# Keeping the split gated outputs of the left half of an output projection for the right half

## Chip, cores and metric

One core of a Trainium2 chip runs the whole kernel in one launch. The metric is the device time of one execution in microseconds (us); lower is better. Engines are named as in the profile: PE (TensorE, matmuls), PEld (its weight loads), DVE (VectorE), ACT (ScalarE), POOL (GpSimd), SP (SyncE, which here issues the DMAs).

## What is computed

A backbone of four layers over 1024 latent tokens and 256 context tokens of width 1024, all in float32. Cut to what matters here:

```python
for i in range(DEPTH):                      # 4 layers, mixers A, B, C, A
    need_ctx = i < DEPTH - 1
    h = rms_norm(x, norm_g[i]) * (1.0 + sc[:, None]) + sh[:, None]
    u, z = jnp.split(h @ w_in, [n_mix_cols], axis=-1)
    ...
    o, oc = mixer(u, uc, ...)               # attention of one of three kinds
    x = x + gt[:, None] * ((o * jax.nn.silu(z)) @ w_out)
    if need_ctx:
        xc = xc + gtc * ((oc * jax.nn.silu(zc)) @ w_out)
```

The last line pair is the output projection: the gated mixer output `o * silu(z)`, 1024 features for each token, times `w_out` (1024 x 1024), times a gate, added to the residual.

## The kernel before

Matmuls run in a reduced float32 form (`F32R`) with each operand split into a high part, rounded to that form, and a low part, the rest. A product is three matmuls: high by high, high by low, low by high (`PROD`, line 372). A split costs one rounding on POOL (`round_pool`, line 130) and one subtraction on DVE (`sub`, line 133).

Every layer has the same stages: projection of the normalised rows to queries, keys, values and gates; attention; output projection (`out_proj`, line 861), which also makes the normalised and modulated rows of the next layer. A layer's gated outputs lie in blocks `og`, features in the partitions. The projection treats tiles of 128 tokens: ten in the first three layers (eight of latent tokens, two of context), eight in the last. It goes through the list `work` (line 904): first the left 512 output columns (h = 0) of all tiles, then the right 512 (h = 1) of all tiles. For each entry:

- `start(i + 1)` splits the gated output of the next entry's tile into two buffers `ogt` (high, low; `parts`, line 901, `split`, line 885), in four blocks: four roundings on POOL, four subtractions on DVE.
- `load` brings the residual rows `xo`, two entries ahead.
- `products` (line 894) runs 24 matmuls of 512 columns into one PSUM bank `y`: eight slices of features by three products.
- With h = 1, in the layers but the last, the transposes of the tile before (`transposed`, line 287, eight matmuls `xT` from `xn`) and its modulation (`modulate`, line 297) follow: four operations `hs` on ACT, four on DVE, then the split of the result for the next layer, `hhi` on POOL and `hlo` on DVE.
- The tile's end: `yg` (DVE, line 934) multiplies by the gate, POOL adds the residual (line 935), a DMA stores it. With h = 1 `norm_rows` (line 279) then squares and sums the rows on ACT (`junk`, line 284), takes the power -1/2 on POOL (`rsqrt`, `rstd`, lines 140 and 146) and scales on DVE (`xn`, line 285).

After the fourth entry from the end the first weights of the next layer are loaded (`wraw`), and split behind the last products (`whi` on POOL, `wlo` on DVE). The transposes of the last tile come after the first pair of the next layer's projections (`proj`, line 382).

Buffers in SBUF come from two pools: 42 "whole" buffers of 1024 elements a partition and 12 "half" ones of 512. A scheduler gives out buffers and sets each engine's order from the order of the code; the function `in_order` pins parts of it. Each engine works its own queue in order.

Of the kernel before, what the change touches and what calls it, by code (L numbers as in the profile page):

```python
# [22 lines left out]
KT = D // P  # L23
# [49 lines left out]
class Net:  # L73
# [787 lines left out]
    def out_proj(self, l, wop, steps, og, tiles):  # L861

        nc = self.nc
        last = l == self.depth - 1
        gts, late = {}, []
        self.new_h()
        new = {t: self.block_rows(self.out, t) if last else self.dram([P, D], name="xres") for t in tiles}

        def load(h, t):
            s = 0 if t < 8 else 1  # L870
            cs = slice(h * 512, h * 512 + 512)
            if s not in gts:
                gts[s] = self.slot([P, D], name="gt")
                g = self.gate[l]
                self.dma(gts[s], bass.AP(tensor=g.tensor, offset=g.offset + s * D, ap=[[0, P], [1, D]]))
            if h == 0 or last:
                full = x = self.slot([P, 512], name="xo")
            else:
                full = self.slot([P, D], name="xo")
                self.dma(full[:, :512], new[t][..., :512])  # L880
                x = full[:, cs]
            self.dma(x, self.xres[t][..., cs])
            return full, x

        def split(t, blocks, ot):

            g, o = t // 4, (t % 4) * P
            for b in blocks:
                a = og.block(b, g)[:, :, o : o + P]
                hi, lo = (x[:, 2 * b : 2 * b + 2, :] for x in ot)  # L890
                self.round_pool(hi, a)
                self.sub(lo, a, hi)

        def products(ps, h, ot, ks):
            for k in ks:
                for j, (a, b) in enumerate(self.PROD):
                    nc.tensor.matmul(  # L897
                        ps, ot[a][:, k, :], wop[h](b, k), start=(k == 0 and j == 0), stop=(k == KT - 1 and j == 2)
                    )

        def parts():
            return [self.slot([P, KT, P], F32R, "ogt") for _ in range(2)]

        work = [(h, t) for h in range(2) for t in tiles]
        ready = [load(*work[0]), load(*work[1])]
        halves = {}

        def start(i):
            ot = parts()
            split(work[i][1], range(4), ot)  # L910
            halves[i] = ot

        start(0)
        for i, (h, t) in enumerate(work):
            cs = slice(h * 512, h * 512 + 512)
            if i < len(steps):
                steps[i]()
            if i + 1 < len(work):
                start(i + 1)
            if i + 2 < len(work):  # L920
                ready.append(load(*work[i + 2]))
            full, x = ready.pop(0)
            ps = self.pb("y")
            products(ps, h, halves.pop(i), range(KT))
            while self.tail:
                self.tail.pop(0)()
            if i + 1 == len(work) and not last:
                for step in splits:
                    step()
            if late:  # L930
                xn, tt = late.pop(0)
                self.modulate(self.transposed(xn), tt, self.mod[l + 1])
            y = self.slot([P, 512], name="yg")
            nc.vector.tensor_tensor(y, ps, gts[0 if t < 8 else 1][:, cs], op=ALU.mult)
            nc.gpsimd.tensor_tensor(x, x, y, op=ALU.add)
            self.dma(new[t][..., cs], x)
            if h == 0 or last:
                continue
            xn = self.slot([P, D], name="xn")
            self.norm_rows(xn, full)  # L940
            late.append((xn, t))
            if i == len(work) - 4:
                self.first_w, loads, splits = self.weight_blocks(*self.first_block(l + 1))
                for x in loads:
                    x()
        self.pending = [
            lambda xn=xn, tt=tt: self.modulate(self.transposed(xn), tt, self.mod[l + 1]) for xn, tt in late
        ]
        for t in tiles:
            self.xres[t] = new[t]  # L950
# [767 lines left out]
```

## Time and profile before

| what | us |
|---|---|
| median of 3 runs | 3666.45 |
| lowest and highest run | 3665.51, 3667.39 |
| the profiled execution, its own time | 3671.03 |
| span of its trace, first to last instruction | 3669.2 |
| PE busy in the span | 3518.5 (96%) |
| DVE, ACT, POOL busy | 2153.7, 1323.0, 1998.8 |

The profile is one execution. A row gives an engine, a line of the kernel, the operation, what it writes and reads (`out<-in`), and times. "Idle before" is the time the engine stood still just ahead of an instruction, with the instruction that ended the wait behind the arrow. The ends of matmuls are modelled, so consecutive matmuls overlap in the rows; their distance in time is read from start to start.

### The profile page before, as it was taken

The numbers are of one execution on the slowest core, as the hardware profiler recorded it, in microseconds if no ns is written. First come the engines' busy times: TensorE is split into PE (matmuls) and PEld (weight loads), VectorE is DVE, ScalarE is ACT, GpSimd is POOL, SyncE is SP. The second block draws the span as 40 slices with busy tenths as digits, with TensorE's granted clock in tenths as the row PEclk, the third lists the DMA queues.
The fourth block names the chain that finished last, engine by engine and source line by source line (L and its number), as shares of the span: only waits on it lengthen the run. The fifth ranks groups of instructions, "written<-read, shape, count | busy, mean of one in ns | idle before, by whom it ended". The sixth has DMA issues, their size and how long they took to land.

```text
span 3669.2 us, 50527 instructions
## 1 busy us (share of the span) xinstructions
PE 3518.5 (96%) x18594; PEld 2615.8 (71%) x18594; DVE 2153.7 (59%) x3675; ACT 1323.0 (36%) x2756; POOL 1998.8 (54%) x2006
## 2 busy tenths in 40 slices
PE   7999999998899999999999999999989999999989
PEld 4887444446788888887778888888877787544447
DVE  5542555565742412888766510899995754566655
ACT  3221444441321212774222211677761221344430
POOL 5540656678631310667765510567776743477786
PEclk9999999999999999999999999999999999999989
DMA  6352543513244444552425432221313334111112
GB/s 208 78 135 83 158 130 103 182 55 97 96 116 138 104 126 111 166 151 69 138 78 137 130 117 61 82 87 38 98 40 99 110 93 125 46 46 37 46 39 86
DMA packets 229459, 370.39 MB, mean 101 GB/s; under 512 B 34088, under 2 KB 124120, under 8 KB 229212
## 3 DMA queue, kind: packets, MB, share of 16 engines
q1 hardware_dynamic: 228636, 367.01, 34.1%
q8 instruction: 148, 2.42, 0.3%
q14 instruction: 99, 0.81, 0.1%
q10 hardware_dynamic: 576, 0.15, 0.0%
HBM read 270.36 MB, written 96.57 MB: 100 GB/s over the span
## 4 chain that ended last, share of the span: by engine, by line
PE 68%; DVE 16%; POOL 9%; issue 4%; DMA 2%; ACT 1%; SPq 0%; POOLq 0%; ACTq 0%; DVEq 0%
PE proj L382 21%; PE zT L467 11%; PE o L725 8%; PE y L897 6%; PE st L700 5%; PE st L701 4%; PE sl L653 3%; DVE ml L1450 3%; PE o L1120 2%; POOL rstd L146 2%; DVE wlo L133 2%; DVE ogt L133 1%; PE qkT L437 1%; POOL hhi L130 1%; POOL p L739 1%
## 5 line engine op out<-in xcount | busy, mean ns | idle before, releaser
L739 POOL TENSOR_TENSOR p<-p,p 128x1024 f32<-128x1024 f32 x224 | 540.1, 2411 | 326.1 <-PE o L725 287.4
L382 PE MATMUL proj<-whi,hhi 128*128 128x512 f32 x1408 | 556.7, 395 | 3.2 <-POOL whi L130 1.9
L382 PE MATMUL proj<-wlo,hhi 128*128 128x512 f32 x1408 | 551.3, 392 | 3.9 <-DVE wlo L133 3.8
L382 PE MATMUL proj<-whi,hlo 128*128 128x512 f32 x1408 | 551.1, 391 | 0.0
L660 DVE TENSOR_REDUCE M<-sl 128x1 f32<-128x512 f32 x512 | 326.8, 685 | 292.5 <-PE sl L653 292.5
L705 ACT ACTIVATE p<-st 128x1024 f32<-128x1024 f32 (+1 forms) x336 | 324.4, 1003 | 314.8 <-PE st L701 303.1
L897 PE MATMUL y<-whi,ogt 128*128 128x512 f32 x1216 | 389.7, 398 | 16.7 <-POOL ogt L130 13.1
L133 DVE TENSOR_TENSOR wlo<-wraw,whi 128x1024 fp32r<-128x1024 f32 x136 | 213.5, 1584 | 217.8 <-POOL whi L130 193.0
L725 PE MATMUL o<-p,v 128*64 128x512 f32 x1344 | 324.5, 605 | 1.7 <-DVE M L660 1.1
L130 POOL TENSOR_SCALAR whi<-wraw 128x1024 fp32r<-128x1024 f32 x136 | 179.0, 1321 | 254.0 <-DMA wraw<-in_c_w_in_dram 91.3
L382 PEld LDWEIGHTS proj<-wlo,hhi 128*128 128x128 f32 x1408 | 265.8, 189 | 58.9 <-DVE wlo L133 6.0
L382 PEld LDWEIGHTS proj<-whi,hhi 128*128 128x128 f32 x1408 | 265.8, 189 | 57.5 <-POOL hhi L130 2.4
L382 PEld LDWEIGHTS proj<-whi,hlo 128*128 128x128 f32 x1408 | 265.6, 189 | 55.4
L897 PEld LDWEIGHTS y<-whi,ogt 128*128 128x128 f32 x1216 | 230.7, 190 | 73.2 <-POOL ogt L130 16.8
L467 PE MATMUL zT<-hhi,whi 128*128 128x512 f32 (+1 forms) x704 | 256.6, 365 | 5.9 <-DVE qklo L133 5.6
L404 ACT ACTIVATE y<-proj 128x1024 f32<-128x1024 f32 (+1 forms) x68 | 65.5, 964 | 527.4 <-PE proj L382 470.0
L467 PE MATMUL zT<-hhi,wlo 128*128 128x512 f32 (+1 forms) x704 | 254.3, 361 | 1.3 <-DVE wlo L133 1.3
L467 PE MATMUL zT<-hlo,whi 128*128 128x512 f32 (+1 forms) x704 | 254.2, 361 | 0.0
L897 PE MATMUL y<-wlo,ogt 128*128 128x512 f32 x608 | 239.6, 394 | 0.0
L146 POOL TENSOR_TENSOR rstd<-rstd,mhalf 128x16 f32<-128x16 f32 (+3 forms) x132 | 230.8, 1748 | 10.9
L700 PE MATMUL st<-q,k 128*128 128x512 f32 x512 | 218.3, 426 | 2.3 <-ACT p L705 2.3
L410 DVE TENSOR_TENSOR y<-y,rstd 128x1024 f32<-128x1024 f32 (+1 forms) x68 | 104.1, 1531 | 193.0 <-POOL rstd L146 193.0
(221 smaller groups left out, 7242.7 us busy)
## 6 DMA issues: line engine op xcount, KB each, us to landing
adaw<-in_ada_w_dram SPq DMA_DIRECT2D x96, 512.0 KB
xo<-xres SPq DMA_DIRECT2D x86, 256.0 KB
wraw<-in_a_w_in_dram SPq DMA_DIRECT2D x40, 512.0 KB
k<-k SPq DMA_DIRECT2D x40, 512.0 KB
q<-qkhi SPq DMA_DIRECT2D x76, 256.0 KB
q<-qklo SPq DMA_DIRECT2D x76, 256.0 KB
q<-q SPq DMA_DIRECT2D x136, 128.0 KB
wraw<-in_b_w_in_dram SPq DMA_DIRECT2D x32, 512.0 KB
```

Of the source, the lines that this page charges most:

```text
L130: self.nc.gpsimd.tensor_scalar(out=out, in0=in_, scalar1=1.0, scalar2=0.0, op0=ALU.mult, op1=ALU.add)
L133: self.nc.vector.tensor_tensor(out, a, b, op=ALU.subtract)
L146: nc.gpsimd.tensor_tensor(r, r, self.mhalf[:, :n], op=ALU.pow)
L382: nc.tensor.matmul(ps[:, i, :], self.h_op(a, 2 * tp + i, k), wop(b, k), start=(k == 0 and j == 0), stop=(k == KT - 1 and j == 2),)
L467: nc.tensor.matmul(ps, wop(a, k)[:, b * P : (b + 1) * P], self.h_cols(c, g, k), start=(k == 0 and j == 0), stop=(k == KT - 1 and j == 2),)
L660: nc.vector.tensor_reduce(out=o, in_=st["ps", hh], axis=AX.X, op=ALU.max)
L700: nc.tensor.matmul(ps[:, hh, :], self.k_op(K, 0, kt), q1[:, hh, :], start=True, stop=False)
L701: nc.tensor.matmul(ps[:, hh, :], self.k_op(K, 1, kt)[0 : HD + 1], q2[:, hh, :], start=False, stop=True)
L705: nc.scalar.activation(p, ps, AF.Exp, scale=HD**-0.5)
L725: nc.tensor.matmul(st["o"][hh * HD : (hh + 1) * HD, :], v(hh, kt), p[:, hh, :], start=j == 0, stop=j == N - 1, tile_position=(0, hh * HD),)
L739: eng.tensor_tensor(a, a, p, op=ALU.add)
L897: nc.tensor.matmul(ps, ot[a][:, k, :], wop[h](b, k), start=(k == 0 and j == 0), stop=(k == KT - 1 and j == 2))
```

## The change

In the left half each tile's split is made once and its two buffers are kept, by the tile's number; the right half reads them again and then lets them go. Ahead of the change each entry of `work` made its own split, so every tile was split twice. For ten tiles up to 20 whole buffers are held at the turn from left to right.

```diff
         def start(i):
-            ot = parts()
-            split(work[i][1], range(4), ot)
-            halves[i] = ot
+
+            t = work[i][1]
+            if t not in halves:
+                halves[t] = parts()
+                split(t, range(4), halves[t])
...
-            products(ps, h, halves.pop(i), range(KT))
+            products(ps, h, halves[t] if h == 0 else halves.pop(t), range(KT))
```

The change's name also speaks of the differential layer's bias; the diff has no line on it. After the change lines from 914 on stand two lower in the file.

The orders of PE and ACT stay as they are. The first place is DVE's queue in the right half of the first layer, between the norm of the third tile and the end of the fourth (`xn`, normalised rows; `ogt`, split of the gated output `og`; `yg`, gated product; `hs`, modulated rows of the tile before). Before:

```order
L285 TENSOR_SCALAR xn_7274<-xo_7080,rstd_7278 128x1024
L133 TENSOR_TENSOR ogt_7283<-og_618,ogt_7282 128x256
L133 TENSOR_TENSOR ogt_7283<-og_621,ogt_7282 128x256
L133 TENSOR_TENSOR ogt_7283<-og_623,ogt_7282 128x256
L133 TENSOR_TENSOR ogt_7283<-og_626,ogt_7282 128x256
L934 TENSOR_TENSOR yg_7347<-y_7295,gt_6603 128x512
L305 TENSOR_SCALAR hs_7330<-xT_7325,colA_589,colS_590 128x128 x4
L133 TENSOR_TENSOR hlo_7178<-hs_7330,hhi_7177 128x2x128
```

The same place now:

```order
L285 TENSOR_SCALAR xn_7234<-xo_7060,rstd_7238 128x1024
L936 TENSOR_TENSOR yg_7297<-y_7245,gt_6603 128x512
L305 TENSOR_SCALAR hs_7280<-xT_7275,colA_589,colS_590 128x128 x4
L133 TENSOR_TENSOR hlo_7148<-hs_7280,hhi_7147 128x2x128
L133 TENSOR_TENSOR hlo_7152<-hs_7280,hhi_7151 128x2x128
```

The four subtractions between `xn` and `yg` are gone; nothing else moved.

The second place is POOL's queue in the same half, from the residual add (`xo`) of the eighth tile on (`rstd`, its norm's factor; `hhi`, the high part of the seventh tile's modulated rows). Before:

```order
L935 TENSOR_TENSOR xo_7446<-xo_7446,yg_7671 128x512
L130 TENSOR_SCALAR ogt_7606<-og_619 128x256 x2
L130 TENSOR_SCALAR ogt_7606<-og_624 128x256 x2
L140 TENSOR_SCALAR rstd_7679<-ss_7677 128x1
L146 TENSOR_TENSOR rstd_7679<-rstd_7679,mhalf 128x1
L130 TENSOR_SCALAR hhi_7493<-hs_7654 128x2x128
L130 TENSOR_SCALAR hhi_7501<-hs_7654 128x2x128
L130 TENSOR_SCALAR hhi_7497<-hs_7654 128x2x128
L130 TENSOR_SCALAR hhi_7505<-hs_7654 128x2x128
L130 TENSOR_SCALAR ogt_7683<-og_619 128x256 x2
L130 TENSOR_SCALAR ogt_7683<-og_624 128x256 x2
```

The same place now:

```order
L937 TENSOR_TENSOR xo_7376<-xo_7376,yg_7581 128x512
L140 TENSOR_SCALAR rstd_7589<-ss_7587 128x1
L146 TENSOR_TENSOR rstd_7589<-rstd_7589,mhalf 128x1
L130 TENSOR_SCALAR hhi_7423<-hs_7564 128x2x128
L130 TENSOR_SCALAR hhi_7431<-hs_7564 128x2x128
L130 TENSOR_SCALAR hhi_7427<-hs_7564 128x2x128
L130 TENSOR_SCALAR hhi_7435<-hs_7564 128x2x128
L937 TENSOR_TENSOR xo_7451<-xo_7451,yg_7645 128x512
```

Two splits of four roundings are gone here. The factor `rstd` of the eighth tile still stands ahead of the `hhi` of the seventh, as it did; at the other tiles `hhi` of the tile before comes first, or three of its four parts.

## Rows read from the trace of the kernel before

**Rows 1.** The page, engines: busy us, share of the span, instructions.

```profile
PE 3518.5 (96%) x18594; PEld 2615.8 (71%) x18594; DVE 2153.7 (59%) x3675; ACT 1323.0 (36%) x2756; POOL 1998.8 (54%) x2006
```

**Rows 2.** Groups of instructions, 923.44 to 1006 us: busy, mean ns, idle before.

```profile
L130 POOL TENSOR_SCALAR ogt<-og 128x256 fp32r<-128x256 f32 x32 | 17.9, 584 | 0.0
```

**Rows 3.** Waits of PE, 923 to 1006 us: total, times, longest.

```profile
PE xT L293 <- DVE xn L285: 9.0, 9, 1.7
```

**Rows 4.** Windows: stretch, length, busy of each engine, PE clock, DMA, GB/s.

```profile
929.67:976.63 46.96, 39.70 (x195) 31.54 (x194) 38.89 (x85) 16.17 (x37) 36.10 (x66) 1.00 0.38 118
976.63:983.75 7.12, 6.78 (x33) 5.20 (x33) 7.12 (x16) 2.30 (x7) 6.30 (x13) 1.00 0.62 225
...
1781.64:1828.61 46.97, 39.66 (x195) 31.54 (x194) 38.89 (x85) 16.17 (x37) 36.11 (x66) 1.00 0.37 119
1828.61:1836.67 8.06, 8.06 (x32) 6.42 (x33) 8.06 (x18) 2.30 (x7) 6.30 (x13) 0.79 0.54 194
...
2834.38:2881.34 46.96, 39.66 (x195) 31.54 (x193) 38.89 (x85) 16.16 (x37) 36.09 (x66) 1.00 0.37 119
2881.34:2888.45 7.11, 6.76 (x32) 5.20 (x33) 7.11 (x16) 2.31 (x7) 6.30 (x13) 1.00 0.60 216
...
3608.80:3663.40 54.60, 54.56 (x241) 44.86 (x239) 24.17 (x42) 0.00 (x0) 29.11 (x40) 1.00 0.31 92
```

**Rows 5.** Timeline of PE, right half of the first layer: start us, us.

```profile
928.65 0.39 PE L897 MATMUL y<-whi,ogt 128*128 128x512 f32 x1
...
929.67 0.48 PE L897 MATMUL y<-whi,ogt 128*128 128x512 f32 x1
...
983.75 0.48 PE L897 MATMUL y<-whi,ogt 128*128 128x512 f32 x1
...
989.09 0.39 PE L897 MATMUL y<-whi,ogt 128*128 128x512 f32 x1
...
1005.03 1.09 PE L293 MATMUL xT<-ident,xn 128*128 128x128 f32 x8 [1.68 <-DVE xn L285]
```

**Rows 6.** Timeline of all engines, 943.1 to 952.6 us.

```profile
943.03 0.39 PE L897 MATMUL y<-whi,ogt 128*128 128x512 f32 x1
...
943.19 0.89 DVE L285 TENSOR_SCALAR xn<-xo,rstd 128x1024 f32<-128x1024 f32 x1
944.01 2.01 DVE L133 TENSOR_TENSOR ogt<-og,ogt 128x256 fp32r<-128x256 f32 x4
...
945.94 0.68 DVE L934 TENSOR_TENSOR yg<-y,gt 128x512 f32<-128x512 f32 x1
...
946.70 1.29 POOL L935 TENSOR_TENSOR xo<-xo,yg 128x512 f32<-128x512 f32 x1 [1.29 <-DVE yg L934]
...
948.02 1.06 ACT L284 ACTIVATE junk<-xo 128x1024 bf16<-128x1024 f32 x1 [1.68 <-POOL xo L935]
...
950.04 0.61 POOL L146 TENSOR_TENSOR rstd<-rstd,mhalf 128x1 f32<-128x1 f32 x1
...
950.68 0.89 DVE L285 TENSOR_SCALAR xn<-xo,rstd 128x1024 f32<-128x1024 f32 x1
```

**Rows 7.** Timelines of ACT, POOL and DVE, 977 to 998 us.

```profile
977.29 1.49 ACT L314 ACTIVATE hs<-xT,colS,colA 128x128 f32<-128x128 f32 x4
...
979.01 1.68 POOL L130 TENSOR_SCALAR hhi<-hs 128x256 fp32r<-128x256 f32 x4
979.82 2.21 DVE L133 TENSOR_TENSOR hlo<-hs,hhi 128x256 fp32r<-128x256 f32 x4
...
988.79 6.45 POOL L130 TENSOR_SCALAR whi<-wraw 128x1024 fp32r<-128x1024 f32 x4
...
990.31 7.56 DVE L133 TENSOR_TENSOR wlo<-wraw,whi 128x1024 fp32r<-128x1024 f32 x4
```

**Rows 8.** The weight loads' issue (timeline of SP), and a window behind them.

```profile
971.26 1.96 SPq L123 DMA_DIRECT2D wraw<-in_b_w_in_dram  x4
...
984.00:992.00 8.00, 6.81 (x33) 5.17 (x32) 7.26 (x13) 3.12 (x9) 7.18 (x10) 1.00 0.09 33
```

## The prediction

> **What bounds the kernel now.** I began with the page: TensorE (PE) is busy for 96% of the span [rows 1], so time can come only from the places where PE stands still, or from shorter PE work; this change takes no matmul away. Next came the groups of instructions in the first layer's right half. GpSimd (POOL) spends 17.9 us there on 32 roundings of the gated output, 584 ns each [rows 2]; the rest of the removed work is as many VectorE (DVE) subtractions. Busy time off PE costs nothing by itself, so the third view is PE's own waits in the same stretch: nine times PE stands before the transposes of a normalised row tile, 9.0 us in all, and each time DVE's `xn` ends the wait [rows 3].
>
> I call the right half's row tiles R0 to R9 (in the last layer R0 to R7). From the start of R2 to the start of R8 each of the first three layers takes 46.96 or 46.97 us for six tiles, 7.83 us a tile [rows 4]. What PE needs for one: from the first to the last of 24 matmuls behind transposes 983.75 to 989.09, 5.34 us; from the last matmul of a tile over eight transposes to the next tile's first, without a wait, 928.65 to 929.67, 1.02 us [rows 5]. That is 6.36 us. So 1.47 us of each tile is idle PE or its restart. The last layer has no norm behind its right half: there PE is busy for 54.56 of 54.60 us although the splits run [rows 4].
>
> The timeline of one tile shows the loop [rows 6]. `xn` of R2 ends at 944.08; DVE then runs four subtractions of the split for 2.01 us; only then, at 945.94, comes `yg` of R3, whose last product had ended at 943.42. From there: POOL adds to the residual (946.70), ACT squares (948.02), POOL's power ends at 950.65, `xn` of R3 ends at 951.57, and one tile later the same subtractions follow. From `yg`'s start to `xn`'s end it is 5.63 us. The loop `xn`, split, `yg`, `xn` closes in 7.49 us (943.19 to 950.68), longer than PE's 6.36.
>
> **The change, part by part.**
>
> *Splits of the right half removed.* 38 tiles (10, 10, 10, 8) times four blocks: 152 roundings on POOL and 152 subtractions on DVE, some 0.58 us and 0.5 us each [rows 2, 6]; 89 and 76 us of engine time, of which only what stands in the loop counts. The last layer's 32 of each go for nothing: PE covers them. In the other layers the loop loses its 2 us on DVE. `yg` can then start when its products end. I add the steps anew for the chain, from the end of a tile's products: `yg` 0.7, add until 2.1, ScalarE's modulation of the tile before until the same 2.1 (its transposes now start together with `yg`), square until 3.4, POOL's four `hhi` until 3.9, `rstd` until 4.8, `xn` until 5.7 to 5.9. PE asks for these transposes 6.36 after the products' end. The chain fits with about 0.5 to spare, and PE becomes the bound. Six intervals at 6.36 are 38.2 us; 46.96 less 38.2 is 8.8 us a layer, three times **26.4 us**.
>
> *One place where it does not fit.* The order rows of POOL show the `rstd` of R7 ahead of the `hhi` of R6, and ScalarE squares R7 before it modulates R6. From the end of R7's products: add until 2.1, square until 3.4, `rstd` until 4.4, four `hhi` (1.68) until 6.1, the last `hlo` (four take 2.21, the last needs the last `hhi`) about 7.0, `xn` 7.9 [rows 7]. PE asks at 6.36 and waits about 1.6. With some 0.2 of restart R8 to R9 takes 8.2 us. It took 7.12, 8.06 and 7.11 [rows 4], so **2.3 us are lost** here. What hid this was the wait of R8 for its split, which goes.
>
> *The end of the layer.* The next layer's weight splits on POOL (`whi`) began at 988.79, 0.7 us before R9's products ended (989.09 plus 0.39) [rows 5, 7]. In the sum above POOL is free for them 12.6 after the end of R7's products, and R9's products end at 14.6, so they begin 2.0 before. The chain behind them (four `whi`, four `wlo` for 7.56 us, then R9's `yg` to `xn`) ends with the transposes at 1005.03, for which PE waits; it moves with them. I take 1.2 us a layer, **3.6 us**.
>
> *Buffers held longer.* Two buffers of 4 KB a partition for each tile stay taken from the left half to the right: 20 of the 42 whole buffers where 4 were. Nothing in the trace of before prices this. Below, it is 0: by the buffer addresses of the built program, the next layer's four weight loads, issued at 971.26 in R7 [rows 8], take buffers last read no later than R6's products. Elsewhere the orders of buffers are as before, but for one load of residual rows in the first layer's left half, which has to wait a microsecond or two longer, for rows used two tiles on. Above, it is the price of the slower rival below. I take 0, since the addresses say so.
> The Trainium skill (Perfetto Trace Analysis, Identifying Performance Opportunities) says that one gap which repeats on the engine that should be saturated can mean too little SBUF for the next tile. By that rule this gap would grow, and the sum would be the slower rival's 3683; the row with `xn` as releaser of all nine waits speaks against it, so I keep the sum below.
>
> *Moved rows.* On POOL one `hhi` and a rope product change places twice; on the SP queue some residual loads pass stores of the same stage. The loads are issued two or three tiles (over 12 us) ahead of their use, and their place changes by one or two issues: 0. PE's and ScalarE's orders are untouched. The title's second half, on the differential layer, has no line in the diff: 0.
>
> *Sum.* 26.4 - 2.3 + 3.6 = 27.7 us. The profiled execution took 3671.03, the median of the runs is 3666.45, 4.6 less; the same work lies in both, so the profiled time would be 3643.3 and the median **3638.8 us**.
>
> **The rivals.**
>
> *More than that, 3626 us.* Every wait in the stretch goes, the end of the layer too. From R2's start to R9's transposes the first layer takes 75.36 us (929.67 to 1005.03). Eight tiles at 6.36 and 48 projection matmuls at 0.23 (5.34 over 23) are 61.9: 13.5 a layer, 40.5 in all. For it: DVE operations may run shorter once POOL has less to do. Against it: the order at R7, and `wlo`'s 7.56 us, both of which stay.
>
> *Half of it, 3652 us.* The chain comes out at 7.0 instead of 5.9, because the modulation of the tile before no longer runs ahead of `yg` and its eight operations and eight splits now queue in the chain. Six intervals at 7.0 plus restart 0.2 save 3.8 a layer, 11.3; plus 3.6 at the layers' ends and less about 1 at R8 that is 14. For it: the overlap with the tile before is new. Against it: at R3 the measured 5.63 already holds the same `hhi` and `hlo` between add and `xn`.
>
> *Slower, 3683 us.* The held buffers run out: the next layer's weight loads wait until R9's products are done. They were issued at 971.26, and the DMA engines were down to a share of 0.09 in 984 to 992 [rows 8], so they take about 13 us. Then `whi` starts 13 us behind the end of R9 in place of 0.7 ahead, and PE has nothing else: 13.7 in three layers, 41, against the 24 gained, 17 us more. It decides from the point where one of the four loads takes a buffer read after R8. For it: the count is near 42 in that stretch. Against it: the addresses.
>
> *No change.* The idle time at the transposes moves to another engine's wait of the same size, or the change does less than its title says. For it: only its first half is in the diff, and PE is at 96%. Against it: the loop above.
>
> **How the numbers follow.** A measurement of this kernel tells about 0.2%, 7.3 us, from no change. Forecast 0.64, more 0.14, half 0.13, no change 0.05, slower 0.04. Faster is the sum of the first three, 0.91; within 0.2% 0.05; slower 0.04. The range goes from the first rival to just past the second, 3626 to 3653; the last two rivals and the far ends lie outside.
>
> **What would show it.** In the changed profile: POOL's and DVE's `ogt` groups at 152 each; PE's waits for `xn` in the first layer's right half down from nine to about two (R7's transposes, about 1.6, and R9's, under 2); R2 to R8 at 38 to 39 us in each of three layers; `yg` starting within 0.1 of its products' end; the last layer's right half still at 54.6. The prediction is wrong if R2 to R8 stays above 42 us (the chain, not the split, was the bound), if PE waits for weights at the next layer's start (buffers), or if the gain appears there and is lost in the next layer's projections.

## The result, and the profile after

The changed kernel took **3636.26 us** (median of 4 runs, 3634.91 to 3639.78) against 3666.76 of the kernel before beside it: ratio 0.9919, 95% interval 0.9902 to 0.9936, 30.5 us less. The profiled execution took 3635.89, its span is 3634.2. The forecast was 3638.8 in a range of 3626 to 3653. One later run, of the kernel that splits the last layer twice, took 11907.82 us and is left out of that kernel's median.

The page of the changed kernel, engines (to set beside [rows 1]):

```profile
PE 3504.5 (96%) x18594; PEld 2615.1 (72%) x18594; DVE 2070.9 (57%) x3523; ACT 1322.5 (36%) x2756; POOL 1918.5 (53%) x1854
```

DVE lost 152 instructions and 82.8 us of busy time, POOL 152 and 80.3. These 163 us bought 30, and the views below say where. First the groups of instructions of the whole span, the split alone (304 of each before):

```profile
L133 DVE TENSOR_TENSOR ogt<-og,ogt 128x256 fp32r<-128x256 f32 x152 | 90.3, 654 | 10.4 <-POOL ogt L130 10.4
L130 POOL TENSOR_SCALAR ogt<-og 128x256 fp32r<-128x256 f32 x152 | 90.1, 620 | 0.0
```

PE's waits in 923 to 1000 us, the first layer's right half and the next layer's start (total, times, longest; before [rows 3]):

```profile
PE xT L293 <- DVE xn L285: 2.8, 2, 1.7
PE proj L382 <- DVE wlo L133: 0.5, 1, 0.5
```

Nine waits became two: before the transposes of R7 and of R9. The windows from R2 to R8 and from R8 to R9 of each of the three layers, and the last layer's whole right half (columns as in [rows 4]):

```profile
924.42:962.54 38.12, 38.12 (x196) 32.01 (x194) 28.04 (x61) 15.80 (x36) 22.81 (x42) 1.00 0.45 137
962.54:970.26 7.72, 6.58 (x35) 5.25 (x34) 4.61 (x11) 2.70 (x7) 3.91 (x8) 1.00 0.66 247
1767.31:1805.42 38.11, 38.11 (x195) 32.00 (x193) 28.03 (x61) 15.80 (x36) 22.82 (x42) 1.00 0.41 137
1805.42:1813.15 7.73, 6.58 (x36) 5.25 (x34) 4.62 (x11) 2.70 (x7) 3.91 (x8) 1.00 0.69 249
2807.73:2845.79 38.06, 38.06 (x195) 31.98 (x194) 28.03 (x61) 15.80 (x36) 22.82 (x42) 1.00 0.43 138
2845.79:2853.53 7.74, 6.55 (x35) 5.26 (x34) 4.62 (x11) 2.70 (x7) 3.92 (x8) 1.00 0.66 245
3584.54:3628.22 43.68, 43.68 (x193) 35.85 (x191) 5.53 (x8) 0.00 (x0) 10.30 (x8) 1.00 0.28 79
```

From R2 to R8 PE's busy time now equals the length of the window: six tiles at 6.35 us with nothing idle. The timeline of one tile, all engines, shows the loop that was 7.49 us long [rows 6]:

```profile
936.15 0.39 PE L897 MATMUL y<-whi,ogt 128*128 128x512 f32 x1
...
936.58 0.69 DVE L936 TENSOR_TENSOR yg<-y,gt 128x512 f32<-128x512 f32 x1 [0.84 <-PE y L897]
...
937.35 1.29 POOL L937 TENSOR_TENSOR xo<-xo,yg 128x512 f32<-128x512 f32 x1 [2.40 <-DVE yg L936]
...
938.67 1.06 ACT L284 ACTIVATE junk<-xo 128x1024 bf16<-128x1024 f32 x1
...
940.69 0.61 POOL L146 TENSOR_TENSOR rstd<-rstd,mhalf 128x1 f32<-128x1 f32 x1
...
941.34 0.76 DVE L285 TENSOR_SCALAR xn<-xo,rstd 128x1024 f32<-128x1024 f32 x1
...
942.71 1.03 PE L293 MATMUL xT<-ident,xn 128*128 128x128 f32 x8
```

DVE now waits for PE (0.84 before `yg`), no longer PE for DVE. `xn` ends at 942.10, 0.6 before PE asks for it at 942.71. The one place that did not fit, R7, from its last product on (the timeline, rows of PE, DVE, POOL and ACT, R6 and R7):

```profile
962.71 1.29 POOL L937 TENSOR_TENSOR xo<-xo,yg 128x512 f32<-128x512 f32 x1 [2.38 <-DVE yg L936]
964.04 1.06 ACT L284 ACTIVATE junk<-xo 128x1024 bf16<-128x1024 f32 x1 [5.19 <-POOL xo L937]
965.09 1.49 ACT L314 ACTIVATE hs<-xT,colS,colA 128x128 f32<-128x128 f32 x4
965.55 0.55 POOL L146 TENSOR_TENSOR rstd<-rstd,mhalf 128x1 f32<-128x1 f32 x1
966.07 1.68 POOL L130 TENSOR_SCALAR hhi<-hs 128x256 fp32r<-128x256 f32 x4
967.42 1.28 DVE L133 TENSOR_TENSOR hlo<-hs,hhi 128x256 fp32r<-128x256 f32 x3 [0.30 <-POOL hhi L130]
968.62 0.74 DVE L285 TENSOR_SCALAR xn<-xo,rstd 128x1024 f32<-128x1024 f32 x1
969.41 1.09 PE L293 MATMUL xT<-ident,xn 128*128 128x128 f32 x8 [1.14 <-DVE xn L285]
973.97 6.46 POOL L130 TENSOR_SCALAR whi<-wraw 128x1024 fp32r<-128x1024 f32 x4
975.60 0.39 PE L897 MATMUL y<-whi,ogt 128*128 128x512 f32 x1
```

R7's factor `rstd` is there at 966.10, but `xn` stands behind `hlo`, `hlo` behind `hhi` of R6, and those behind ACT's `hs`, which queue behind the square of R7. The last two rows show the layer's end: `whi` begins 2.0 before R9's products end.

### The profile page after: what moved, and what is told of

Its sections match the earlier page's. It is cut to its first block, busy times and chain, and to the rows that moved or that the text cites. A ratio compares the mean times of both kernels' runs of the same rounds, so it can differ in the third digit from the quotient of the medians.

```text
span 3634.2 us, 50186 instructions
## 1 busy us (share of the span) xinstructions
PE 3504.5 (96%) x18594; PEld 2615.1 (72%) x18594; DVE 2070.9 (57%) x3523; ACT 1322.5 (36%) x2756; POOL 1918.5 (53%) x1854
## 4 chain that ended last, share of the span: by engine, by line
PE 73%; DVE 13%; POOL 7%; issue 3%; DMA 2%; ACT 1%; SPq 0%; POOLq 0%; DVEq 0%; ACTq 0%
PE proj L382 21%; PE zT L467 12%; PE y L897 9%; PE o L725 8%; PE st L700 5%; PE st L701 4%; PE sl L653 3%; DVE ml L1452 3%; PE o L1122 2%; DVE wlo L133 1%; POOL rstd L146 1%; PE qkT L437 1%; POOL p L739 1%; PE ada L195 1%; PE pT L1200 1%
```

## The experiments

Medians are compared with the changed kernel's 3636.26 us; a second set of its runs, below, gave 3637.50, so a few us between two kernels can't be told from none. The windows tell more: in two traces of the same kernel those of a stretch agree within 0.1. The sets of runs were made on different chips; the kernel before, run beside each of them, took 3666.76, 3667.21, 3668.22 and 3668.25.

**POOL's roundings back.**

```diff
+            elif not last:
+                again = self.slot([P, KT, P], F32R, "oga")
+                for b in range(4):
+                    self.round_pool(again[:, 2 * b : 2 * b + 2, :], halves[t][0][:, 2 * b : 2 * b + 2, :].bitcast(F32))
```

> The changed kernel, with the four POOL roundings per tile of the right half put back (layers 0 to 2) at their old places, from the kept high part into a buffer that nothing reads. Extra work without use: 30 tiles x 4 roundings of 584 ns, 70 us of POOL. Theory (what went from the loop is DVE's four subtractions between xn and yg; POOL's roundings lay beside it): R2 to R8 stays at 38 to 39.5 us a layer, and the time is 0 to 4 us above the changed kernel's. Rival (POOL's queue was the bound, its load of 36.1 us of 47 with the waits in it): R2 to R8 goes back to 44 to 47 us, and the time is 18 to 27 us above the changed kernel's.

3643.13 us, 6.9 above the changed kernel. The window from R2 to R8 of the first layer:

```profile
929.34:967.73 38.39, 38.39 (x195) 31.86 (x194) 29.07 (x61) 15.77 (x36) 32.81 (x63) 1.00 0.44 137
```

Two of its groups of instructions in 925 to 965 us:

```profile
L130 POOL TENSOR_SCALAR oga<-ogt 128x256 fp32r<-128x256 f32 x24 | 12.0, 523 | 0.0
L285 DVE TENSOR_SCALAR xn<-xo,rstd 128x1024 f32<-128x1024 f32 x6 | 5.4, 892 | 3.8 <-POOL rstd L146 3.5
```

Ten us of POOL work came back and the six tiles took 0.3 us more: POOL alone was not the bound, as the theory had it. The time went a little above its 0 to 4: up to R9's transposes the last two layers, whose PE clock is undisturbed, cost 1.1 us each, mostly from R8 to R9 (8.56 for 7.73), and the first 1.2; the other half of the 6.9 is not placed, and can be the spread of the medians. One number was not expected: `xn` takes 0.89 again, as before the change, where the changed kernel has 0.76.

**DVE's subtractions back.**

```diff
+            elif not last:
+                again = self.slot([P, KT, P], F32R, "oga")
+                for b in range(4):
+                    c = slice(2 * b, 2 * b + 2)
+                    self.sub(again[:, c, :], halves[t][1][:, c, :].bitcast(F32), halves[t][0][:, c, :])
```

> The changed kernel, with the four DVE subtractions per tile of the right half put back (layers 0 to 2) between xn and yg, from the kept parts into a buffer that nothing reads. Extra work without use: 30 tiles x 2.0 us of DVE, no POOL work. Theory (these 2.0 us are the loop): the loop xn, subtractions, yg, xn closes in about 7.4 us again, R2 to R8 at 44.5 to 47 us a layer, the time 18 to 26 us above the changed kernel's. Rival (POOL's load was the bound): R2 to R8 at 38 to 40 us, the time within 5 us of the changed kernel's.

3660.53 us, 24.3 above: inside the theory's range. The stage says otherwise. The window from R2 to R8:

```profile
929.37:970.53 41.16, 39.46 (x196) 31.56 (x194) 34.86 (x84) 15.78 (x36) 23.01 (x43) 1.00 0.40 122
```

The timeline of DVE at one tile:

```profile
948.24 0.75 DVE L285 TENSOR_SCALAR xn<-xo,rstd 128x1024 f32<-128x1024 f32 x1
948.90 1.43 DVE L133 TENSOR_TENSOR oga<-ogt,ogt 128x256 fp32r<-128x256 f32 x4
...
955.00 0.75 DVE L285 TENSOR_SCALAR xn<-xo,rstd 128x1024 f32<-128x1024 f32 x1
```

PE's waits in 970 to 1003 us, the layer's end:

```profile
PE xT L293 <- DVE xn L285: 4.7, 3, 3.6
```

41.16, not 44.5 to 47: the loop closes in 6.76 (948.24 to 955.00, the next `xn`), not in 7.4. The four subtractions take 1.43 in place of 2.01 [rows 6], `xn` 0.75 in place of 0.89. Only 9.2 of the 24.3 us are in the six tiles of the three layers. About 12 more lie at the layers' ends: there DVE's order came out another way (R8's `yg` behind the `hlo` of R7), and PE waits 3.6 before R8's transposes. So the total agreed with the theory for a reason that is not the theory's.

**Both back, neither waiting for the other.** The two pieces above together, each into a buffer of its own.

> The changed kernel, with both the four POOL roundings and the four DVE subtractions per tile of the right half back (layers 0 to 2), but both from the kept parts into buffers that nothing reads, so that no subtraction waits for a rounding. Extra work without use. With the subtractions alone R2 to R8 was 41.16, with the roundings alone 38.4, before the change 46.97. In the subtraction run a subtraction stood at 0.34 us from the next and xn took 0.75; before the change 0.53 and 0.89, with roundings running on POOL at the same time. Theory A (DVE's operations take longer while POOL rounds): R2 to R8 at 45 to 47 us, subtractions 0.6 us long, xn 0.89. Theory B (before the change the subtractions waited for their own roundings): R2 to R8 at 41 to 42.5 us, subtractions 0.42 us.

One run: 3672.53 us. The window from R2 to R8:

```profile
924.05:969.62 45.57, 39.45 (x196) 31.54 (x194) 39.23 (x86) 15.79 (x36) 34.72 (x64) 1.00 0.36 109
```

The timeline of POOL and DVE at one tile:

```profile
952.56 2.28 POOL L130 TENSOR_SCALAR ogb<-ogt 128x256 fp32r<-128x256 f32 x4
952.62 0.90 DVE L285 TENSOR_SCALAR xn<-xo,rstd 128x1024 f32<-128x1024 f32 x1
953.43 2.01 DVE L133 TENSOR_TENSOR oga<-ogt,ogt 128x256 fp32r<-128x256 f32 x4
```

`xn` 0.90 and the subtractions 2.01: the numbers of before within a hundredth [rows 6], though no subtraction reads a rounding here. Theory A holds: DVE's operations stretch while POOL rounds. The subtractions alone cost the six tiles 3.0 us (41.16 less 38.12), the roundings alone 0.3, both 7.5. The 1.4 us short of 46.97 lie between R7 and R8 (7.17 for 8.62). There, before the change, R8's products waited for the split of their own tile; here they read kept parts. The row of the trace of before:

```profile
976.63 0.50 PE L897 MATMUL y<-whi,ogt 128*128 128x512 f32 x1 [1.22 <-POOL ogt L130]
```

The Trainium skill (SBUF — State Buffer, SBUF: two separate sides) says that DVE and GpSimd share one pair of ports as an exclusive lock, which a DVE operation in a two-port mode needs, or one with two SBUF inputs beside a GpSimd operation that reads SBUF, and the GpSimd operation too; whoever comes second is blocked for the whole instruction. The trace agrees that each slows the other: a subtraction and a rounding side by side start 0.53 us after the last pair (four in 2.01), while subtractions alone start 0.34 apart (four in 1.43). It comes nearest to a whole block beside POOL's residual add (at 969.39, 1.40 us): a subtraction that starts at 969.56 takes 1.51 there in place of 0.42, and ends 0.29 behind the add. A subtraction and a rounding overlap in part: roundings with no subtraction or `xn` beside them start 0.37 apart (in the run with POOL's roundings alone, at 947.49 and 947.86), and one after the other a pair would take 0.71, not 0.53.

**The last layer split twice.**

```diff
-            if t not in halves:
+            if t not in halves or last:
...
-            products(ps, h, halves[t] if h == 0 else halves.pop(t), range(KT))
+            products(ps, h, halves[t] if h == 0 else halves[t], range(KT))
```

> The changed kernel, but the last layer splits its eight tiles a second time in the right half, as before the change: 32 roundings and 32 subtractions back, 18.7 and 16 us of engine time. Theory (PE covers them, as no norm stands behind this half): the last layer's right half stays within 0.2 us of its 54.6, and the time within 2 us of the changed kernel's. Rival (removed work is worth the same everywhere): a tile there costs 1.4 us more, 8 to 11 us in all.

3633.40 us (three runs), 2.9 below. Its right half, R0 to the end, and behind the dots that of the kernel before:

```profile
3580.91:3624.59 43.68, 43.68 (x193) 35.87 (x191) 13.30 (x22) 0.00 (x0) 18.27 (x20) 1.00 0.35 103
...
3619.72:3663.40 43.68, 43.64 (x193) 35.81 (x191) 13.25 (x23) 0.00 (x0) 18.19 (x20) 1.00 0.35 103
```

43.68 as without them (3584.54:3628.22 above), to the hundredth, and as before the change. (The stretch of 54.60 in [rows 4], which the expectation means, begins two tiles ahead of the right half.) The last layer's share of the removed work was worth nothing.

**Buffers held longer.** The first form put a memset on four buffers at R0 and another at the right half's last tile.

```diff
+        held = []
...
+            if not last and i in (len(tiles), len(work) - 1):
+                held = held or [self.slot([P, D], name="held") for _ in range(4)]
+                for x in held:
+                    nc.gpsimd.memset(x[0:1, :16], 0.0)
```

> The changed kernel, with four more whole buffers held from the first tile of the right half to its last (layers 0 to 2), by small memsets on POOL at both ends. Nothing else is changed. Theory A (my slower rival's mechanism is near: of 42 buffers few are in reserve): one or more of the next layer's four weight loads, or loads of residual rows, is issued later than R7, and the time rises by 3 to 25 us. Theory B (a reserve of four or more is there): the loads are issued in R7 as they are, and the time stays within 2 us of the changed kernel's.

3635.77 us, 0.5 below, and it shows nothing: the second memset depends on no late data, so the scheduler put both side by side (24 memsets of 0.1 us on POOL, eight in 1.3 us in each layer), and the built program gives the four buffers two addresses in turn. Nothing was held. The second form ties the end to R9's gated row:

```diff
...
+            if not last and i + 1 == len(work):
+                for v in held:
+                    nc.gpsimd.tensor_tensor(v[0:1, :16], v[0:1, :16], y[0:1, :16], op=ALU.add)
```

> The same with four buffers held. Reuse moves by up to one tile. Theory: within 3 us of the changed kernel's, the weight loads issued within 1 us of it. Rival: 3 to 10 us more.

> The changed kernel with six whole buffers more held over the right half (layers 0 to 2): a tiny memset at R0, and a tiny add of R9's gated row on POOL at the end, which can't run before R9's products are done. By the buffer addresses of the built program each reuse moves half a tile to one tile closer: the residual load of R4 takes a buffer last read in R3 in place of R2, and the next layer's weight loads take buffers last read between R7.6 and R8.0 in place of R6.5 to R7.0. Extra work: 18 memsets and 18 small adds, under 0.3 us each. Theory (loads have slack): weight loads issued 1 to 3 us later, R2 to R8 within 0.3 us of 38.1, no new wait; the time within 4 us of the changed kernel's. Rival (my slower case decides near here): residual or weight loads arrive late, PE waits for them, 5 to 17 us more.

Four held: 3637.63 us in one run, R2 to R8 38.18, the four weight loads issued 4.5 to 0.8 us ahead of R8's start (4.4 to 2.9 without). The time is as the theory says; the last load comes 2.1 us later, more than the 1 us that it allowed. Six held: **3670.87 us**, 34.6 above the changed kernel and 33.2 above the one run with four beside it, twice the rival's upper end. Of six, the windows from R2 to R8 and from R8 to R9:

```profile
927.11:971.19 44.08, 38.51 (x196) 31.85 (x193) 29.71 (x61) 15.80 (x36) 22.86 (x42) 1.00 0.31 98
971.19:982.59 11.40, 7.36 (x36) 6.03 (x34) 4.57 (x11) 3.08 (x8) 4.71 (x8) 0.85 0.73 248
```

PE's waits in 923 to 1000 us:

```profile
PE xT L293 <- DVE xn L285: 9.6, 3, 4.0
```

The timeline of POOL, PE and DVE behind R2's products:

```profile
932.45 0.39 PE L897 MATMUL y<-whi,ogt 128*128 128x512 f32 x1
932.70 0.41 POOL L130 TENSOR_SCALAR hhi<-hs 128x256 fp32r<-128x256 f32 x1 [1.81 <-PE y L897]
933.48 0.41 DVE L133 TENSOR_TENSOR hlo<-hs,hhi 128x256 fp32r<-128x256 f32 x1
933.93 1.63 DVE L285 TENSOR_SCALAR xn<-xo,rstd 128x1024 f32<-128x1024 f32 x1
935.62 1.09 PE L293 MATMUL xT<-ident,xn 128*128 128x128 f32 x8 [2.78 <-DVE xn L285]
```

What came late is no load, the one thing that theory and rival weighed: by the built program's addresses the last `hhi` of R0 takes a buffer that R2's last products read, so POOL waits for PE (1.81). R1's `xn` stands behind it on DVE, and PE pays 2.78 before R1's transposes. It is the same behind R6 and R8, in each layer. The three layers lose 9.5, 12.7 and 11.1 us up to R9's transposes, 33.3 of the 34.6. The reserve beside the 20 held buffers is thus at least four and under six.

**The order at R7, and at the layer's end.** The first edit pins ACT's and POOL's order around `modulate` and `norm_rows` (`pin`); the second also writes out DVE's and POOL's order at the last tile (`both`):

```diff
+        chain = {}
+        pin = lambda f: self.in_order(f, chain, (nc.scalar.engine, nc.gpsimd.engine))
...
-                self.modulate(self.transposed(xn), tt, self.mod[l + 1])
+                pin(lambda: self.modulate(self.transposed(xn), tt, self.mod[l + 1]))
...
-            self.norm_rows(xn, full)
+            pin(lambda: self.norm_rows(xn, full))
```

```diff
+        ends = {}
+        both = lambda f: self.in_order(f, ends, (nc.vector.engine, nc.gpsimd.engine))
...
+            if end:
+                both(splits[0])
...
+                both(lambda: nc.vector.tensor_tensor(y, ps, gts[0 if t < 8 else 1][:, cs], op=ALU.mult))
+                both(splits[1])
+                both(lambda: nc.gpsimd.tensor_tensor(x, x, y, op=ALU.add))
...
+                both(splits[2])
+                both(splits[3])
+                both(lambda: self.norm_rows(xn, full))
+                xt, tt = late.pop(0)
+                self.modulate(self.transposed(xt), tt, self.mod[l + 1])
```

> The changed kernel again, unchanged, beside the two pinned versions on the same chip, so that they can be compared with it: 3633 to 3641 us, R2 to R8 at 38.1, R8 to R9 at 7.73.

> The changed kernel, with ACT's and POOL's order pinned so that a tile's modulation (hs, hhi) stands ahead of the next tile's norm (square, rstd) at R7 too. Nothing is left out. Theory (the order makes the wait at R7's transposes): the wait of 1.14 to 1.18 goes, R8 to R9 falls from 7.73 to 6.4 to 6.6, and the time by 3 to 4.5 us. Rival (the wait is there for another reason, or PE gives it back in the next layer's start): R8 to R9 falls but the distance from R2 to the transposes of R9 stays, and so does the time, within 1.5 us. A sharper form of the rival: those transposes end behind weight splits whose start is bound to the hhi, so half of it may be lost.

> The one before, and the layer's end pinned too: yg of R9 stands behind the first of the four weight splits wlo on DVE in place of the last, the residual add and the norm of R9 between the others, and R8's modulation behind them. Nothing is left out. Theory (R9's transposes are late because yg of R9 queues behind four wlo of 7.56 us): the wait at R9's transposes of 1.7 us goes in each of three layers; together with the pin at R7 the time falls by 7 to 10 us against the changed kernel, to about 3627 us. Rival (the late wlo then delay the next layer's first projections instead): a wait for wlo of 1 to 3 us a layer takes its place, and the time is no lower than with the first pin alone.

The changed kernel again: 3637.50 us (4 runs, 3636.87 to 3639.48), R2 to R8 38.13, 38.07 and 38.04.

The first pin: 3636.83 (3633.38 to 3638.43), 0.7 less. Window R8 to R9 of the first layer:

```profile
964.89:971.22 6.33, 6.33 (x35) 5.33 (x33) 4.82 (x11) 2.70 (x7) 3.96 (x7) 1.00 0.83 306
```

The wait at R7 is gone and R8 to R9 is 6.33: the order made it. But from R2 to R9's transposes the layers gain only 0.91, 0.85 and 0.77 where R7's interval gains 1.40, and the median moves by less than it can tell. The sharper rival was right: the layer's end takes part of it back.

Both pins: **3632.09 us** (4 runs, 3628.32 to 3633.57), ratio to before 0.9898, 0.9884 to 0.9912. That is 5.4 below the changed kernel beside it, and all four runs lie under all eight of that kernel. PE's waits in 923 to 1000 us, and, behind the dots, in 1800 to 1900 us:

```profile
PE proj L382 <- DVE wlo L133: 0.9, 2, 0.6
PE xT L293 <- DVE xn L285: 0.2, 1, 0.2
...
PE proj L382 <- DVE wlo L133: 3.5, 3, 2.6
```

R9's transposes come 2.1, 3.1 and 3.0 us sooner after R2, 8.3 in all. Not all of it lasts. Where the second layer's end gave 5.1 us (a start of 1833.61 for 1838.72 in the first projections), 4.1 are gone by 1891: at 1887.08 PE waits 2.57 for a `wlo` of the next weights, and behind the wait its granted clock is low for 3 us (7 matmuls, clock 0.52):

```profile
1887.08:1890.16 3.08, 3.08 (x7) 2.46 (x8) 3.08 (x3) 0.00 (x0) 0.85 (x1) 0.52 0.96 268
```

The first layer's gain, 1.8 us at 1250, is 0.4 at 1451, lost in the attention for a reason that is open; the third layer's stays. In these two traces 3.4 us are left at the last output projection. Theory and rival share it: the medians show 5.4 of the expected 7 to 10 us, and of the rest only the second layer's wait for weights is shown.

## Why the prediction was right

**What bounds.** The loop `xn`, split, `yg`, `xn` was the bound and PE took its place. R2 to R8 is 38.12, 38.11 and 38.06 for 38.2 predicted: 26.6 us gained for 26.4. The chain from a tile's products to the end of `xn` took 5.6 us (936.54 to 942.10) for 5.7 to 5.9, so PE's own 6.35 is the longer.

**R7.** The mechanism and the order are as predicted; the size was not. The term said a wait of 1.6 and 8.2 us for R8 to R9, it is 1.14 and 7.73. From the end of R7's products (961.51 plus 0.39) `rstd` was there after 4.2 us, not 4.4, and `xn` ended 0.66 behind the last `hlo`, not 0.9: half of the difference each. `xn` was costed at 0.89, the row of a tile with POOL's roundings beside it; without them it is 0.74, and R7's own `xn` in the trace of before (at 973.51) took 0.75. The loss is 0.9 us in three layers, not 2.3. What had hidden it was R8's wait for its split, as predicted: 1.22 in the row at 976.63 above, a tenth wait of PE beside the nine of [rows 3].

**The layer's end.** 1.2 us a layer predicted; from R9's start to its transposes 21.28, 22.07 and 22.28 became 19.96, 20.96 and 20.96: 1.3, 1.1 and 1.3, together 3.75 for 3.6.

**Sum.** 26.6 - 0.9 + 3.75 = 29.45 us, where the sum said 27.7; the medians differ by 30.5, and the 1 us between is less than they can tell. The two profiled executions differ by 35.1, but 6.1 of that is already there at the first output projection (859.94 before, 853.80 after), which the change does not touch. That start lies at 853.66, 856.38 and 858.81 in the runs with the last layer split twice, the changed kernel again and the memsets: it varies by itself.

**Buffers.** The term 0 is right: the four weight loads were issued from 958.11 to 959.66, in R7, and PE's one wait for weights is 0.5 us (0.6 before the change). The rival was nearer than it looked: with six buffers fewer the kernel is as slow as before, though through `hhi` and not through late loads. Also the argument against the Trainium skill's rule (Perfetto Trace Analysis, Identifying Performance Opportunities: a repeating gap can mean too little SBUF) was too weak. I held the releaser `xn` of all nine waits [rows 3] against it. With six buffers held the gap is a shortage of buffers, and PE's wait still names `xn`. The evidence stands one step upstream: there POOL's `hhi` waits for PE's `y`; before the change the subtractions of `ogt` fill the time between `xn` and `yg` [rows 6].

**What the prediction did not see.** It priced the loop's gain as the 2 us of DVE's subtractions. They are 1.4 us by themselves; the rest of the 2.0, and 0.14 of `xn`, is POOL's rounding at the same time. The forecast came out since both go together and PE bounds the rest: the bound was understood, the price of its parts was luck.

**Nothing elsewhere.** The last layer gave 0, as said. The row that the prediction read for it (54.56 of 54.60 us) holds ten tiles, the last two of the left half with the right half; the right half alone is 43.68 before and after, so the reading holds. The rivals of more (3626) and half (3652) did not come.

## What to carry to other kernels

Where the busiest engine waits, follow the loop of the engine that ends the wait, close it in microseconds, and stop the gain where the next engine's own time begins: 82.8 us of DVE and 80.3 of POOL were worth 30 us, nearly all of it in three stretches. Price an operation from a row with the same neighbours as it will have: DVE's rows beside a busy POOL were up to 40% too long. Before holding buffers for longer, tie up a few more by a use that can't run early, and see where the time breaks.

## What was not expected of the hardware

DVE and POOL slowed each other: four subtractions 1.43 us alone and 2.01 beside roundings, `xn` 0.75 and 0.89. A subtraction beside POOL's residual add took 1.51 for 0.42.

After a wait of PE of some 2.6 us the granted clock was sometimes low, sometimes not. The window of 4 us from R9's transposes in the second layer, in the changed kernel (a wait of 2.67 ahead):

```profile
1834.11:1838.11 4.00, 4.00 (x15) 3.41 (x16) 1.43 (x5) 3.27 (x6) 3.15 (x4) 0.57 0.60 133
```

The same with the first pin (a wait of 2.63 ahead):

```profile
1834.15:1838.15 4.00, 4.00 (x22) 3.45 (x23) 1.49 (x5) 3.28 (x6) 3.31 (x4) 1.00 0.63 135
```

0.57 is mostly the lower of the clock's two levels, 1.2 of 2.4 GHz: 15 matmuls in place of 22. The changed kernel shows both by itself: after the third layer's wait of 2.7 us the 4 us had 0.66 in its first trace and 1.00 in its second. The shorter waits at R7 (1.14 to 1.19) were not followed by it. What decides is open.
